# One load cut in two, and the last stores dealt out to other DMA engines, in a float32 matmul with bias and residual

## The chip, the cores and the metric

The kernel runs on 1 core of one Trainium2 chip. The metric is device time in microseconds (us), median of several runs. A ratio is the mean time of one kernel's runs over the mean of the other's runs of the same rounds, so it is not quite the ratio of the medians that are quoted beside it; it comes with a 95% interval.

A word on names. PE is the matmul engine, PEld its weight loads, DVE, ACT and POOL the vector, scalar and GpSimd engines, SP the queue that issues every transfer here. The *16 DMA engines* are the machines that move the bytes. A *landing* is the moment at which one of them adds its one to a transfer's semaphore: an evenly spread transfer has 16 of them, and the trace keeps their times, though not the engine's number.

## The reference

```python
x: (16, 512, 1024)  weight: (1024, 768)  bias: (768,)  residual: (16, 512, 768)   # float32
return np.matmul(x, weight) + bias + residual                                     # float32
```

The core must read 61.9 MB and write 25.2 MB; the profile's own account says so.

## The kernel before

The 8192 rows are 64 tiles of 128 rows, eight tiles to a *super tile* (S = 0 to 7). A row is on partition p and slot j, so a whole super tile of x (4 MB), residual or output (3 MB) moves in one transfer, with one long run of bytes per partition. A tile is cast to bf16 (ACT), transposed on PE, copied out of PSUM (DVE), multiplied, and added to residual and bias in place in the residual's buffer, from which it is stored. All transfers are issued by SP in the order of one list:

```python
# (kind, S, j0, j1[, cut]): x load, r residual load, s store, c store of one column chunk of one tile
ORDER = [('x', 0, 0, 2), ('w', 0, 0, 2), ...                                   # cut
 ('x', 1, 1, 4), ('r', 0, 4, 8), ('x', 1, 4, 8), ('r', 1, 2, 6), ('x', 2, 0, 8), ('r', 1, 6, 8),
 ...                                                                            # cut
 ('r', 6, 0, 8), ('s', 3, 0, 8), ('x', 7, 0, 8), ('r', 7, 0, 8), ('s', 4, 0, 8), ('s', 5, 0, 8), ('s', 6, 0, 8),
 ('s', 7, 3, 4, 108), ('s', 7, 0, 3), ('s', 7, 4, 6), ('s', 7, 6, 7), ('c', 7, 7, 0), ('c', 7, 7, 1)]
```

A store with a `cut` is issued as two transfers, the rows before and after it (here and in e12 below the wrapper `K_`, which keeps the order of the program, is left out):

```python
edges = [0, *cut, P]                       # P = 128
for p0, p1 in zip(edges, edges[1:]):
    nc.sync.dma_start(out=out_d[S, p0:p1, j0:j1, n0:n0 + nl],
                      in_=R[S % RO_SLOTS][p0:p1, j0:j1, n0:n0 + nl])
```

So before, tile 59 (S = 7, j = 3) is stored as 108 rows and 20 rows. The Trainium skill, "DMA: Bandwidth & Descriptors", section "Why a DMA increments its semaphore by 16 and not by 1", says that a transfer runs on k engines, k being the largest number up to 16 that divides its slowest dimension, and on the lowest-numbered k; an issuing sequencer writes the other 16 - k increments at once. The trace agrees on k: the 108-row store shows one early update and then 12 landings, the 20-row one 1 and 10. Thus 108 rows go as 9 rows to each of engines 0 to 11, 20 rows as 2 to each of 0 to 9, and engines 12 to 15 get no row of that tile. I call that *relief*: an even store gives every engine 8 rows. The numbers 0 to 15 here are labels by this rule; no trace prints them.

Of the kernel before, what the change touches and what calls it, by code (L numbers as in the profile page):

```python
# [28 lines left out]
 ('fin', 0), ('mm', 1, 3), ('mm', 2, 3)]  # L29
ORDER = [('x', 0, 0, 2), ('w', 0, 0, 2), ('x', 0, 2, 4), ('w', 1, 0, 2), ('b', 0, 0, 0), ('w', 2, 0, 2),  # L30
 ('w', 3, 0, 2), ('x', 0, 4, 6), ('r', 1, 0, 2), ('x', 0, 6, 8), ('r', 0, 0, 4), ('x', 1, 0, 1),
 ('x', 1, 1, 4), ('r', 0, 4, 8), ('x', 1, 4, 8), ('r', 1, 2, 6), ('x', 2, 0, 8), ('r', 1, 6, 8),
 ('r', 2, 0, 8), ('x', 3, 0, 8), ('s', 0, 0, 8), ('r', 3, 0, 8), ('x', 4, 0, 8), ('r', 4, 0, 8),
 ('s', 1, 0, 8), ('x', 5, 0, 8), ('r', 5, 0, 8), ('s', 2, 0, 8), ('x', 6, 0, 8), ('r', 6, 0, 8),
 ('s', 3, 0, 8), ('x', 7, 0, 8), ('r', 7, 0, 8), ('s', 4, 0, 8), ('s', 5, 0, 8), ('s', 6, 0, 8),
 ('s', 7, 3, 4, 108), ('s', 7, 0, 3), ('s', 7, 4, 6), ('s', 7, 6, 7), ('c', 7, 7, 0),
 ('c', 7, 7, 1)]
LAST = [(0, 512), (512, 256)]

# [256 lines left out]
```

## Time and profile before

| | before |
|---|---|
| median (range, runs) | 210.86 us (210.71 to 211.16, 6 runs) |
| span in the profile | 208.9 us |
| PE busy | 96% |
| DMA queue q1, share of 16 engines | 98.1% |
| last vector add ends | 204.8 us |
| landings of the very last store | 206.49 to 207.81 us |

Lines of the page of the kernel before: the span, the engines' busy time, the DMA engines' busy tenths and GB/s in 40 slices, the queues (packets, MB, share), and the chain that ended last, by engine.

```profile
span 208.9 us, 3104 instructions
...
PE 201.1 (96%) x1273; PEld 130.1 (62%) x1298; DVE 104.9 (50%) x140; ACT 67.2 (32%) x69; POOL 116.0 (56%) x72
...
DMA  6999999999999999999999999999999999999995
GB/s 234 426 429 413 415 434 436 418 457 404 443 430 460 398 419 441 453 408 431 424 433 435 438 433 409 463 424 411 452 414 439 414 433 441 428 428 420 419 395 205
...
q1 hardware_dynamic: 5918, 87.05, 98.1%
q8 instruction: 10, 0.16, 0.3%
q14 instruction: 4, 0.03, 0.0%
...
PE 76%; DMA 18%; ACT 1%; DVE 1%; issue 1%; SPq 0%; ACTq 0%
...
```

Two things are full at once: PE, and the DMA engines, whose row of tenths is 9 everywhere but at the two ends. 417 GB/s (87.05 MB in 208.9 us) fits the Trainium skill, "Perfetto Trace Analysis", section "Roofline", which puts a core alone at about 435 GB/s by its 16 DMA engines. The queue q8 is ten packets of 16 KB that are instructions, 0.3% of the time. (Queue q14 has four more in the span, of 8 KB and 0.3 us each.)

The place that the first half of the change aims at, in the timeline of the kernel before (start, us, engine, what; in brackets the idle time before it and who ended it), and in the waits between 40 and 60 us (in total, times, longest):

```profile
...
54.62 2.94 ACT L148 CAST xb<-x_tile 128x1024 bf16<-128x1024 f32 x3 [9.51 <-DMA x_tile<-in_x_dram]
55.72 0.42 PEld L156 LDWEIGHTS pt<-ident,xb 128*128 128x128 f32 x4 [0.48 <-ACT xb L148]
55.72 0.66 PE L156 MATMUL pt<-ident,xb 128*128 128x128 f32 x4
...
```

```profile
...
ACT xb L148 <- DMA x_tile<-in_x_dram: 15.2, 2, 9.5
...
PEld pt L156 <- ACT xb L148: 0.5, 1, 0.5
```

The cast of tile 16 waits until 54.62 us for the whole 4 MB of x of super tile 2, so PE's transposes start at 55.72 us. PE's transposes had come every 3.04 us (49.39, 52.43), so they were due at 55.47: 0.25 us late (0.3 at the next ones). No later wait of PE is of this kind.

The place that the second half aims at, the tail in the table of stretches of the kernel before (stretch in us, its length, busy times, granted clock, then DMA share and GB/s), and its small stores (KB each, us from issue to landing):

```profile
...
core 0: us, PE busy (x) PEld busy (x) DVE busy (x) ACT busy (x) POOL busy (x), PEclk, DMA share, GB/s
...
205.00:206.00 1.00, 0.00 (x0) 0.00 (x0) 0.00 (x0) 0.00 (x0) 0.00 (x0) 1.00 0.92 357
206.00:207.00 1.00, 0.00 (x0) 0.00 (x0) 0.00 (x0) 0.00 (x0) 0.00 (x0) 1.00 0.56 205
207.00:208.00 1.00, 0.00 (x0) 0.00 (x0) 0.00 (x0) 0.00 (x0) 0.00 (x0) 0.98 0.07 25
208.00:209.00 1.00, 0.00 (x0) 0.00 (x0) 0.00 (x0) 0.00 (x0) 0.00 (x0) 0.50 0.00 0
...
```

```profile
...
out_dram<-ro SPq DMA_DIRECT2D x1, 1152.0 KB, 8.0
out_dram<-ro SPq DMA_DIRECT2D x1, 768.0 KB, 5.2
...
out_dram<-ro SPq DMA_DIRECT2D x1, 384.0 KB, 4.1
out_dram<-ro SPq DMA_DIRECT2D x1, 324.0 KB
out_dram<-ro SPq DMA_DIRECT2D x1, 256.0 KB, 3.2
out_dram<-ro SPq DMA_DIRECT2D x1, 128.0 KB, 3.0
out_dram<-ro SPq DMA_DIRECT2D x1, 60.0 KB
...
```

After 204.8 us there is nothing left but stores, and the DMA share falls off gently: 0.92, 0.56, 0.07. If all 16 engines ended together it would fall at once. They do not, and the landings of the last store say how far apart they are (read from the trace, in order of time):

```
last store, before: 206.49 206.50 206.51 206.52 206.55 206.57 206.65 206.75 206.77 207.05 207.28 207.29 207.38 207.71 207.73 207.81
```

The lag is older than the tail. Here are landings of four big transfers, each 16 equal parts, with the 16 KB fetches that came between (the store of S=4, which lies between the second and the third, is left out):

```
x of S=7:        168.78 to 168.91 (4), 169.29 to 169.83 (4), 170.15 to 170.37 (7), 170.65
      16 KB instruction fetch at 176.7
residual of S=7: 176.08 to 176.21 (4), 176.59 to 177.13 (4), 177.44 to 177.65 (7), 179.45
store of S=5:    190.62 to 190.71 (4), 191.14, 191.15, 191.95 to 192.32 (9), 194.04
      16 KB instruction fetch at 196.3
store of S=6:    197.88 to 197.95 (4), 198.38, 198.39, 199.20 to 199.85 (8), 200.88, 201.28
```

Over the run the landings show eight engines that get such a jump, of about 1.5 us, one after each of the first eight fetches, and stay behind; the fetches at 176.7 and 196.3 us fall on two of these, which end 3.0 and 3.4 us behind the first (200.88 and 201.28 against 197.88). They are the *twice-hit* engines of this text. By following packets (chaining each to the one whose end meets its start) I found that all 16 engines run without a gap from 2 us to about 197 us at the earliest, 203.5 us for most, so a lag is not made up before the tail.

### The profile page before, as it was taken

The page shows a single profiled execution, that of the slowest core. Times are in us where ns is not written, and L with a number is a line of the kernel's source. Part 1 is how long each engine was busy: PE and PEld are TensorE (multiplying, and loading weights), DVE is VectorE, ACT ScalarE, POOL GpSimd, SP SyncE. Part 2 cuts the span into 40 slices and gives each one's busy share as a digit, 9 for nine tenths or more (in the row PEclk, how much of TensorE's full clock was granted, in tenths as well). Part 3 has the DMA queues.
Part 4 walks back from the last instruction along what each step waited for, and adds up shares of the span by engine and source line. Part 5 has one row for each costly group of instructions (what it writes and reads, how often), then busy time and mean ns, then how long its engine had stood idle before and what let it go on. Part 6 is the DMA issues. An engine that isn't in the chain of part 4 may idle for free.

```text
span 208.9 us, 3104 instructions
## 1 busy us (share of the span) xinstructions
PE 201.1 (96%) x1273; PEld 130.1 (62%) x1298; DVE 104.9 (50%) x140; ACT 67.2 (32%) x69; POOL 116.0 (56%) x72
## 2 busy tenths in 40 slices
PE   7999999999999999999999999999999999999991
PEld 2455666666666666666666666666666666666660
DVE  0457555427454644464554455455445544544551
ACT  2444325160563062422443054230724234430000
POOL 2100069999257990199589802994059910699100
PEclk9999999999999999999999999999999999999999
DMA  6999999999999999999999999999999999999995
GB/s 234 426 429 413 415 434 436 418 457 404 443 430 460 398 419 441 453 408 431 424 433 435 438 433 409 463 424 411 452 414 439 414 433 441 428 428 420 419 395 205
DMA packets 5932, 87.24 MB, mean 418 GB/s; under 512 B 666, under 2 KB 794, under 8 KB 2206
## 3 DMA queue, kind: packets, MB, share of 16 engines
q1 hardware_dynamic: 5918, 87.05, 98.1%
q8 instruction: 10, 0.16, 0.3%
q14 instruction: 4, 0.03, 0.0%
HBM read 61.88 MB, written 25.17 MB: 417 GB/s over the span
## 4 chain that ended last, share of the span: by engine, by line
PE 76%; DMA 18%; ACT 1%; DVE 1%; issue 1%; SPq 0%; ACTq 0%
PE psum_o L163 64%; DMA x_tile<-in_x_dram 18%; PE pt L156 11%; PE psum_o L257 1%; ACT xb L148 1%; DVE xt L157 1%; ACT xb L145 0%; DVE ro L261 0%; SPq L118 0%; SPq L121 0%; ACTq L148 0%
## 5 line engine op out<-in xcount | busy, mean ns | idle before, releaser
L163 PE MATMUL psum_o<-w_sb,xt 128*128 128x256 bf16 (+1 forms) x983 | 172.7, 324 | 1.7 <-DVE xt L157 0.3
L163 PEld LDWEIGHTS <-xt 128*128 128x128 bf16 x1008 | 98.5, 98 | 59.1 <-DVE xt L157 0.7
L188 POOL TENSOR_TENSOR ro<-ro,bias_sb 128x768 f32<-128x768 f32 x56 | 99.7, 1818 | 52.3 <-DMA ro<-in_residual_dram 52.3
L148 ACT CAST xb<-x_tile 128x1024 bf16<-128x1024 f32 x60 | 60.8, 1044 | 113.0 <-DMA x_tile<-in_x_dram 62.7
L157 DVE COPY xt<-pt 128x1024 bf16<-128x1024 bf16 x64 | 44.0, 691 | 76.9 <-PE pt L156 76.8
L198 DVE TENSOR_TENSOR ro<-psum_o,ro 128x768 f32<-128x768 f32 x55 | 52.3, 950 | 12.3 <-POOL ro L188 11.0
L156 PE MATMUL pt<-ident,xb 128*128 128x128 f32 x256 | 38.4, 274 | 0.3 <-ACT xb L145 0.2
L156 PEld LDWEIGHTS pt<-ident,xb 128*128 128x128 f32 x256 | 29.7, 141 | 9.3 <-ACT xb L145 1.1
L184 POOL TENSOR_TENSOR ro<-ro 128x768 f32<-128x768 f32 x8 | 14.3, 1822 | 19.4 <-DMA ro<-in_residual_dram 19.4
L194 DVE TENSOR_TENSOR ro<-psum_o,bias_sb 128x768 f32<-128x768 f32 x8 | 7.5, 948 | 0.0
L207 PE MATMUL psum_o<-warm 128*128 128x512 bf16 x12 | 5.3, 629 | 1.2 <-DVE warm_a L203 1.2
L228 ACT CAST w_sb<-ro 128x768 bf16<-128x768 f32 x4 | 3.3, 832 | 3.7 <-DMA ro<-in_weight_dram 3.7
L207 PEld LDWEIGHTS <-warm 128*128 128x128 bf16 x12 | 1.6, 141 | 4.0 <-issue 2.8
L228 POOL CAST w_sb<-ro 128x768 bf16<-128x768 f32 x1 | 0.8, 822 | 5.5 <-DMA ro<-in_weight_dram 5.5
L148 DVE CAST xb<-x_tile 128x1024 bf16<-128x1024 f32 x1 | 0.7, 696 | 4.4 <-DMA x_tile<-in_x_dram 4.4
L145 ACT CAST xb<-x_tile 128x512 bf16<-128x512 f32 x3 | 1.8, 616 | 3.4 <-PE psum_o L163 1.7
L257 PE MATMUL psum_o<-w_sb,xt 128*128 128x512 bf16 (+1 forms) x16 | 2.8, 326 | 0.0
L228 DVE CAST w_sb<-ro 128x768 bf16<-128x768 f32 x3 | 1.7, 558 | 2.0 <-DMA ro<-in_weight_dram 2.0
L146 DVE CAST xb<-x_tile 128x512 bf16<-128x512 f32 x3 | 1.2, 425 | 2.6 <-DMA x_tile<-in_x_dram 2.6
L257 PEld LDWEIGHTS <-xt 128*128 128x128 bf16 x16 | 1.6, 98 | 1.1
L222 PE MATMUL psum_o<-warm 128*128 128x512 bf16 x6 | 1.6, 379 | 0.0
L261 DVE TENSOR_TENSOR ro<-psum_o,ro 128x512 f32<-128x512 f32 (+1 forms) x2 | 1.1, 558 | 0.9 <-PE psum_o L257 0.8
(14 smaller groups left out, 5.1 us busy)
## 6 DMA issues: line engine op xcount, KB each, us to landing
x_tile<-in_x_dram SPq DMA_DIRECT2D x6, 4096.0 KB, 31.0
out_dram<-ro SPq DMA_DIRECT2D x7, 3072.0 KB, 24.7
ro<-in_residual_dram SPq DMA_DIRECT2D x6, 3072.0 KB, 21.4
ro<-in_residual_dram SPq DMA_DIRECT2D x3, 1536.0 KB, 22.2
x_tile<-in_x_dram SPq DMA_DIRECT2D x4, 1024.0 KB, 10.9
ro<-in_weight_dram SPq DMA_DIRECT2D x4, 768.0 KB, 9.7
x_tile<-in_x_dram SPq DMA_DIRECT2D x1, 2048.0 KB, 25.6
ro<-in_residual_dram SPq DMA_DIRECT2D x2, 768.0 KB, 21.5
```

What stands on the lines that cost most here:

```text
L145: K_(nc.scalar.copy(out=dst[:, 0:K // 2], in_=src[:, 0:K // 2]))
L148: K_((nc.scalar.copy if how == "s" else nc.vector.tensor_copy)(out=dst, in_=src))
L156: K_(nc.tensor.transpose(out=pt[:, q, :], in_=words[:, ts(q, P)], identity=ident))
L157: K_(nc.vector.tensor_copy(out=XT[t % XT_N].rearrange("p q m e -> p (q m e)"), in_=pt.rearrange("p q m -> p (q m)").bitcast(BF16),))
L163: K_(nc.tensor.matmul(PO[t % HEAD][:, n0:n0 + nl], lhsT=XT[t % XT_N][:, q, :, e], rhs=w_sb[:, q, e, n0:n0 + nl], start=(q == 0 and e == 0) ...
L184: K_(nc.gpsimd.tensor_add(out=r, in0=r, in1=tmp(t)))
L188: K_(nc.gpsimd.tensor_add(out=r, in0=r, in1=bias_sb))
L194: K_(nc.vector.tensor_add(out=tmp(t), in0=p, in1=bias_sb))
L198: K_(nc.vector.tensor_add(out=row(t), in0=p, in1=row(t)))
L207: K_(nc.tensor.matmul(PO[0][:, 0:512], lhsT=warm[:, 0:P], rhs=warm, start=True, stop=True))
L228: K_(copy(out=w_sb[:, q, e, :], in_=w_st[:, 2 * q + e, :]))
L257: K_(nc.tensor.matmul(p, lhsT=XT[t % XT_N][:, q, :, e], rhs=w_sb[:, q, e, n0:n0 + nl], start=(q == 0 and e == 0), stop=(q == n_q - 1 and e ...
```

## The change

Its intent: let PE begin super tile 2 when the first quarter of x is there; and spare two DMA engines more rows of the last stores. Tile 59 goes with tiles 56 to 60 in one even store, and tiles 61 and 62 are each stored as 126 rows and 2 rows. By the k rule 126 rows go as 9 to each of engines 0 to 13, and 2 rows as 1 to each of engines 0 and 1 (not to 14 and 15).

```diff
- ('x', 1, 1, 4), ('r', 0, 4, 8), ('x', 1, 4, 8), ('r', 1, 2, 6), ('x', 2, 0, 8), ('r', 1, 6, 8),
+ ('x', 1, 1, 4), ('r', 0, 4, 8), ('x', 1, 4, 8), ('r', 1, 2, 6), ('x', 2, 0, 2), ('x', 2, 2, 8),
+ ('r', 1, 6, 8),
  # cut: unchanged transfers, moved to other lines
- ('s', 7, 3, 4, 108), ('s', 7, 0, 3), ('s', 7, 4, 6), ('s', 7, 6, 7), ('c', 7, 7, 0),
+ ('s', 6, 0, 8), ('s', 7, 0, 5), ('s', 7, 5, 6, 126), ('s', 7, 6, 7, 126), ('c', 7, 7, 0),
  ('c', 7, 7, 1)]
```

No instruction of PE, DVE, ACT or POOL changes or moves; SP issues one transfer more.

## The prediction

> **What bounds the kernel now.** Two resources, both full. The page shows PE 96% busy and DMA queue q1 at 98.1% of the 16 engines' span, 417 GB/s. The chain of waits is almost all PE from 54.6 us on, but the end is a DMA: the last vector add ends at 204.8 us, the last store lands at 207.8, the span is 208.9.
>
> I followed packets in the trace, chaining each to the one whose end meets its start. Each of the 16 engines runs back to back from 2 us to about 203.5 us. They are not equally late: the store of super tile 6 ends between 197.4 and 200.9 us depending on the engine. The lag comes from ten 16 KB instruction fetches, each costing its engine about 1.35 us; two engines were hit twice. The last store lands on its engines between 206.5 and 207.8 us. The early ones wait for PE and the issue; the late ones were never idle.
>
> **x of super tile 2 in two transfers.** In the timeline the scalar cast at 54.62 us waits for the whole 4 MB of x (issued 24.5, landed 54.5), and the next transposes start about 0.3 us late against the 3.04 us tile pace; this is the only PE gap after the head. The first quarter lands some 7 us earlier, so the wait goes. PE, and both last stores' issue, move 0.3 us earlier. The late DMA engines do not care: their bytes are the same. One more issue (0.33 us on SP) and 8 more packets per engine cost almost nothing.
>
> **The tail stores.** The Trainium skill, "DMA: Bandwidth & Descriptors", section "Why a DMA increments its semaphore by 16 and not by 1", says a DMA uses the largest k up to 16 that divides its slowest dimension, on the lowest-numbered k engines. The trace agrees on k (the 108-row store lands in 12 steps, the 20-row one in 10); which engines, it does not show. So now, against an even 8 rows, engines 12-15 are spared 8 rows; after, 14-15 are spared 16, but 12-13 carry 18 rows instead of 16. One 3,072-byte row takes 118 ns. Against before: engines 2-9 lose a row (-0.1 us), 0-1 and 10-11 gain one, 14-15 lose 8 (-0.9), 12-13 gain 10 (+1.2 us).
>
> Which of 12-15 are late decides it. By row counts, among them are one engine never hit, one hit once, and the two hit twice, ending at 206.9 and 207.4 us. Fetches six and seven seem to fall on 10 and 11, eight to ten then on 12, 13, 14. If so the latest engine is 13: it ends 1.2 us later, and the kernel at 212.0. If the two are 14 and 15, the change saves 0.2 to 0.5 us. I hold the first likelier, 2 to 1.
>
> **Prediction.** 211.7 us, 8 in 10 between 210.2 and 212.3. Faster by over 2%: 0.01; within 2%: 0.97; slower by over 2%: 0.02.
>
> **What the profile should show.** No cast wait near 54.6 us, PE ending 0.3 us earlier; the 126-row stores landing in 14 steps, the 2-row ones in 2; the last store's 16 landings wider apart, the last near 209.0 against 207.8.
>
> **What would make it wrong.** The twice-hit engines being 14 and 15; fetches falling on other engines in the new program; the five-row store (issued at 197.7 us) leaving early engines dry; slow issue of small-k stores (the 20-row one took 0.89 us, the next 1.52) delaying the last two.

(The prediction's times of single engines are ends of packets. A landing comes a little later: the last packet of the kernel before ends at 207.40 us, its last landing is at 207.81.)

## The result, and the profile after

211.88 us (211.48 to 212.2, 6 runs) against 210.86; ratio 1.0046, interval [1.0031, 1.006]. The change makes the kernel slower by half a per cent, about 1 us, within the range forecast.

The page of the changed kernel, the same lines:

```profile
span 210.0 us, 3104 instructions
...
PE 200.2 (95%) x1273; PEld 130.0 (62%) x1298; DVE 104.8 (50%) x140; ACT 67.3 (32%) x69; POOL 116.0 (55%) x72
...
DMA  6999999999999999999999999999999999999994
GB/s 231 428 421 418 414 438 435 412 457 399 434 462 424 423 435 424 426 443 407 435 448 429 426 417 426 446 421 437 431 426 451 424 414 434 445 409 426 392 373 174
...
q1 hardware_dynamic: 5912, 87.05, 97.8%
q8 instruction: 10, 0.16, 0.3%
...
PE 88%; DMA 7%; SPq 2%; issue 1%; ACT 0%; DVE 0%; ACTq 0%
...
```

The totals hardly move; the DMA row's last digit is 4 instead of 5, the last slice 174 GB/s instead of 205. The first half of the change, in the timeline and the waits of the changed kernel between 40 and 60 us:

```profile
...
47.58 1.99 ACT L148 CAST xb<-x_tile 128x1024 bf16<-128x1024 f32 x2 [2.31 <-DMA x_tile<-in_x_dram]
...
54.89 2.94 ACT L148 CAST xb<-x_tile 128x1024 bf16<-128x1024 f32 x3 [5.32 <-DMA x_tile<-in_x_dram]
55.56 0.47 PEld L156 LDWEIGHTS pt<-ident,xb 128*128 128x128 f32 x4
55.67 0.60 PE L156 MATMUL pt<-ident,xb 128*128 128x128 f32 x4
...
```

```profile
...
ACT xb L148 <- DMA x_tile<-in_x_dram: 13.3, 3, 5.6
...
```

The first two tiles are cast at 47.58 us, long before they are needed; PE waits for no cast here (the line of PEld is gone from the waits) and the transposes come at 55.67, on the pace (49.60, 52.64). In this profile the head had been 0.2 us later, so the last PE work ends only 0.1 us earlier. The chain agrees: the DMA share of it fell from 18% to 7% and PE's rose from 76% to 88%, and yet the time grew. So the chain's shares do not say what the end waits for.

The tail, and the small stores:

```profile
...
core 0: us, PE busy (x) PEld busy (x) DVE busy (x) ACT busy (x) POOL busy (x), PEclk, DMA share, GB/s
...
205.00:206.00 1.00, 0.00 (x0) 0.00 (x0) 0.00 (x0) 0.00 (x0) 0.00 (x0) 1.00 0.88 309
206.00:207.00 1.00, 0.00 (x0) 0.00 (x0) 0.00 (x0) 0.00 (x0) 0.00 (x0) 0.62 0.87 330
207.00:208.00 1.00, 0.00 (x0) 0.00 (x0) 0.00 (x0) 0.00 (x0) 0.00 (x0) 0.50 0.44 161
208.00:209.00 1.00, 0.00 (x0) 0.00 (x0) 0.00 (x0) 0.00 (x0) 0.00 (x0) 0.50 0.07 24
...
```

```profile
...
out_dram<-ro SPq DMA_DIRECT2D x1, 1920.0 KB, 8.3
...
out_dram<-ro SPq DMA_DIRECT2D x2, 378.0 KB
...
out_dram<-ro SPq DMA_DIRECT2D x1, 256.0 KB, 4.4
out_dram<-ro SPq DMA_DIRECT2D x1, 128.0 KB, 4.1
out_dram<-ro SPq DMA_DIRECT2D x2, 6.0 KB
...
```

Between 206 and 208 us the DMA engines are now at 0.87 and 0.44 where they were at 0.56 and 0.07: the same bytes end later and further apart. The landings of the last store:

```
last store, after:  207.31 207.33 207.35 207.36 207.38 207.40 207.61 207.65 207.74 207.87 207.90 208.21 208.27 208.40 208.82 208.91
```

The last is 1.10 us later than before (208.91 against 207.81), which is the whole loss: the span grew by 1.1 us (208.9 to 210.0). The 126-row stores show 14 landings after one early update, the 2-row ones 2 after one. The 16 are a little wider apart, 1.60 us against 1.32, because the early landings are later too, by 0.8 us; whether that matters is asked below.

### The profile page after: what moved, and what is told of

It reads as the page before. It is cut to its first block, busy times and chain, and to the rows that moved or that the text cites. A ratio compares the mean times of both kernels' runs of the same rounds, so it can differ in the third digit from the quotient of the medians.

```text
span 210.0 us, 3104 instructions
## 1 busy us (share of the span) xinstructions
PE 200.2 (95%) x1273; PEld 130.0 (62%) x1298; DVE 104.8 (50%) x140; ACT 67.3 (32%) x69; POOL 116.0 (55%) x72
## 4 chain that ended last, share of the span: by engine, by line
PE 88%; DMA 7%; SPq 2%; issue 1%; ACT 0%; DVE 0%; ACTq 0%
PE psum_o L163 74%; PE pt L156 13%; DMA x_tile<-in_x_dram 7%; PE psum_o L257 1%; SPq L118 1%; SPq L121 0%; SPq L112 0%; ACT xb L145 0%; DVE ro L261 0%; ACTq L145 0%
## 5 line engine op out<-in xcount | busy, mean ns | idle before, releaser
L207 PE MATMUL psum_o<-warm 128*128 128x512 bf16 x12 | 4.6, 557 | 1.2 <-DVE warm_a L203 1.2
L222 PE MATMUL psum_o<-warm 128*128 128x512 bf16 x6 | 1.6, 379 | 0.0
```

What stands on the lines that cost most here:

```text
L207: K_(nc.tensor.matmul(PO[0][:, 0:512], lhsT=warm[:, 0:P], rhs=warm, start=True, stop=True))
```

## The experiments

Theory L (load): the end is the landing of the latest DMA engine; of the two twice-hit engines one is number 13, which the old cut spared 8 rows and the new one loads with 18 instead of 16. Its rivals: X, the cut load of x costs; I, the small stores on fewer than 16 engines are slow to issue, and this delays the end; H, the twice-hit engines are 14 and 15. All experiments change only the list of transfers, except the last.

| kernel | median us (runs) | ratio to before, interval | last landings in its profile |
|---|---|---|---|
| changed kernel | 211.88 (6) | 1.0046 [1.0031, 1.006] | 208.82, 208.91 |
| e1_x_only | 211.1 (5) | 1.0006 [0.9993, 1.0018] | 207.97, 208.04 |
| e2_tail_only | 212.17 (5) | 1.0051 [1.0036, 1.0065] | 208.22, 208.59 |
| e3_even | 211.74 (5) | 1.0033 [1.0021, 1.0046] | 208.50, 208.52 |
| e4_117 | 211.64 (5) | 1.0028 [1.0014, 1.0042] | 208.37, 208.50 |
| e6_before_even | 211.95 (6) | 1.0046 [1.0029, 1.0064] | 208.38, 208.58 |
| e7_112_16 | 211.63 (5) | 1.0037 [1.0024, 1.0051] | 208.22, 209.00 |
| e8_s6_126x2 | 211.65 (5) | 1.0043 [1.003, 1.0056] | 207.87, 208.82 |
| e9_s6_117 | 210.63 (5) | 0.9994 [0.9981, 1.0006] | 207.64, 207.75 |
| e10_s6_126 | 211.71 (5) | 1.0045 [1.0033, 1.0058] | 207.83, 209.02 |
| e11_s6_117x2 | 211.73 (6) | 1.001 [0.9986, 1.0035] | 207.88, 207.93 |
| e12_shift | 212.02 (4) | 1.0029 [1.0014, 1.0043] | 208.37, 208.51 |

The kernel before ran at 210.97 to 210.98 us beside e1 to e6, at 210.76 beside e7 to e10, and at 211.49 (210.69 to 211.76) beside e11 and e12, whose chip was slower and scattered more; compare by ratio. Each profile is one execution, often not the one with the median time. In these executions the device time is 2.7 to 3.2 us above the last landing, for both kernels and for all runs of the table: the time follows the last landing.

### e1_x_only and e2_tail_only: each half alone

```diff
 # e1, from before                      # e2, from before
-('x', 2, 0, 8)                         -('s', 7, 3, 4, 108), ('s', 7, 0, 3), ('s', 7, 4, 6), ('s', 7, 6, 7)
+('x', 2, 0, 2), ('x', 2, 2, 8)         +('s', 7, 0, 5), ('s', 7, 5, 6, 126), ('s', 7, 6, 7, 126)
```

> The kernel before with only x of super tile 2 split in two. Theory L (load: the span ends when the latest of the 16 DMA engines has moved its bytes, and the latest one, hit by two instruction fetches, is one of 12 and 13, which lost their relief): the split takes the 0.3 us PE wait near 54.6 us away but gives no time back, 210.6 to 210.9 us, ratio 0.998 to 1.000. Rival X (the split is what costs, by one more transfer and shifted semaphores): 211.5 to 212 us, ratio about 1.004.

> The kernel before with only the new tail stores. Theory L: 211.9 us, ratio 1.004 to 1.006, as the changed kernel. Rival X: 210.6 to 211.0. Rival I (the small-k stores issue slowly and delay the last two stores): also 211.9, so this run tells X from the other two only.

Measured: 1.0006 and 1.0051. The tail is the whole loss and rival X falls. In e1 the second-last store is issued at 203.99 us against 204.25 before: PE did gain its 0.26 us, and the kernel got nothing for it, because the last landing (208.04, against 207.81 in the profile of before) is that of an engine that had bytes to move anyway.

### e3_even: the changed kernel without any small store

```diff
-('s', 7, 5, 6, 126), ('s', 7, 6, 7, 126)
+('s', 7, 5, 6), ('s', 7, 6, 7)
```

> The changed kernel with tiles 61 and 62 stored evenly as 128 rows on 16 engines, no small-k store left. Theory L: engine 13 carries 16 rows instead of 18, 0.24 us less: 211.5 to 211.8 us, ratio about 1.0035. Rival I (issue of the small-k stores costs the microsecond): the loss is gone, 210.5 to 210.9 us. Rival H (the twice-hit engines are 14 and 15, which now lose a relief of 16 rows): 212.5 us or more unless those were not last.

Measured: 1.0033, as L said; rival I, for which the loss should be gone, falls as the explanation of most of it, and the 212.5 us or more of rival H did not come (211.74). The landings are the cleanest picture of the lags, because every engine carries the same:

```
last store, e3_even: 206.17 206.18 206.20 206.22 206.25 206.37 206.66 206.69 206.72 206.73 206.76 206.78 206.88 207.72 208.50 208.52
```

Thirteen engines end by 206.9, a *third latest* at 207.7, the two twice-hit ones at 208.5. Here is what the cuts are for.

### e6_before_even: the kernel before without its relief

```diff
-('s', 7, 3, 4, 108)
+('s', 7, 3, 4)
```

> The kernel before with tile 59 stored evenly as 128 rows on 16 engines, the relief taken away and nothing else. Theory L: engines 12 to 15 carry 8 rows more (0.93 us), the others up to 3 fewer: 211.5 to 211.8 us, ratio 1.003 to 1.0045. Rival I: small-k stores gone, issue faster (the 20-row one took 0.89 us, the next 1.52): 210.4 to 210.8 us.

Measured: 1.0046, just above the 1.003 to 1.0045 that L expected. The last two landings are 208.38 and 208.58, the third 207.61, the others at most 206.84. So the old cut was worth the microsecond: it takes the twice-hit two from 208.5 to 207.8, and pays with later ordinary engines. One transfer fewer and no small-k store did not help: rival I falls again.

### e4_117: the relief for three engines, in the tail

```diff
-('s', 7, 5, 6, 126), ('s', 7, 6, 7, 126)
+('s', 7, 5, 6, 117), ('s', 7, 6, 7, 117)
```

> The changed kernel with tiles 61 and 62 each stored as 117 rows on 13 engines and 11 rows on 11, which spares engines 13, 14 and 15 of 16 rows. Theory L with engine 13 the latest: engine 13 carries 18 rows less than in the changed kernel, and the latest is then one of the ordinary engines with one row more than in the kernel before: 210.6 to 211.1 us, ratio 0.999 to 1.001. Theory L with engine 12 the latest: no gain, 211.8 us. Rival I: four small-k stores remain, no gain, 211.8 to 212.2 us.

Measured: 1.0028: a miss. About four tenths of the loss seem recovered (1.0046 to 1.0028), but the two intervals overlap. The landings tell that the twice-hit engines were not last: their part of the five-row store landed at 205.89 and 205.99 us, 9 rows more take 1.06 us (9 x 118 ns), and no landing of the 117-row store is later than 206.06; so neither of the two was among its 13 engines. Other engines ended at 208.5. My sum had two holes: the third latest engine is not spared by this cut and carries 20 rows instead of 16 (4 x 118 ns = 0.47 us on its 207.7), and two pairs of small stores in the tail make everything later. (In this trace three packets of the five-row store, started after 202 us, took 1.10 to 1.40 us; the usual time is 0.57.) e11 below has the same rows without such pairs.

### e9_s6_117 and e10_s6_126: relief given earlier, to engines 13 to 15 or to 14 and 15

Both store super tile 7 evenly and cut one tile of super tile 6 instead, in a store that is issued at 182.2 us and lands near 200 us.

```diff
 # from e3
-('s', 6, 0, 8)
+('s', 6, 0, 7), ('s', 6, 7, 8, 117)        # e9;  e10 has 126
```

> Super tile 6 stored as seven tiles evenly and one tile as 117+11 rows, super tile 7 evenly; engines 13 to 15 are spared 8 rows, early enough that no small-k store is in the tail. Theory L with engine 13: the twice-hit two go from 208.5 to 207.6 us, and the third latest engine (207.7 with even stores) gets 2 rows and ends near 207.95: 210.9 to 211.1 us, ratio 0.999 to 1.001. With engine 12 twice hit instead: no gain, 211.7 to 212.0 us.

> As e9 but the one tile as 126+2 rows, which spares 14 and 15 alone. Theory L with engine 13: it keeps all its rows and gets one more, last landing about 208.6 us, 211.7 to 211.9 us, ratio 1.0035 to 1.0045. Rival H (14 and 15 twice hit): as e9, 210.8 to 211.1 us.

Measured: 0.9994 and 1.0045. This is the decisive pair: two kernels with the same number of transfers, the same shape of tail and nearly the same rows; the one difference that counts is whether engine 13 is spared. Rival H, that 14 and 15 are the twice-hit ones, falls. The tail of e9, then of e10, in the table of stretches:

```profile
...
core 0: us, PE busy (x) PEld busy (x) DVE busy (x) ACT busy (x) POOL busy (x), PEclk, DMA share, GB/s
...
205.00:206.00 1.00, 0.00 (x0) 0.00 (x0) 0.00 (x0) 0.00 (x0) 0.00 (x0) 1.00 0.99 383
206.00:207.00 1.00, 0.00 (x0) 0.00 (x0) 0.00 (x0) 0.00 (x0) 0.00 (x0) 1.00 0.46 168
207.00:208.00 1.00, 0.00 (x0) 0.00 (x0) 0.00 (x0) 0.00 (x0) 0.00 (x0) 1.00 0.04 14
208.00:209.00 1.00, 0.00 (x0) 0.00 (x0) 0.00 (x0) 0.00 (x0) 0.00 (x0) 0.56 0.00 0
...
```

```profile
...
core 0: us, PE busy (x) PEld busy (x) DVE busy (x) ACT busy (x) POOL busy (x), PEclk, DMA share, GB/s
...
205.00:206.00 1.00, 0.00 (x0) 0.00 (x0) 0.00 (x0) 0.00 (x0) 0.00 (x0) 1.00 0.97 377
206.00:207.00 1.00, 0.00 (x0) 0.00 (x0) 0.00 (x0) 0.00 (x0) 0.00 (x0) 0.67 0.62 233
207.00:208.00 1.00, 0.00 (x0) 0.00 (x0) 0.00 (x0) 0.00 (x0) 0.00 (x0) 0.50 0.11 39
208.00:209.00 1.00, 0.00 (x0) 0.00 (x0) 0.00 (x0) 0.00 (x0) 0.00 (x0) 0.50 0.05 16
...
```

In e10 the DMA engines are still at 0.05 in the last microsecond, about one engine of 16, and the landings show that it is one alone:

```
last store, e9_s6_117:   206.22 206.25 206.26 206.27 206.29 206.37 206.79 206.83 206.84 206.87 207.10 207.12 207.18 207.43 207.64 207.75
last store, e10_s6_126:  206.29 206.31 206.32 206.34 206.55 206.63 206.71 206.92 207.28 207.37 207.38 207.40 207.47 207.58 207.83 209.02
```

The cut stores say the same directly: the 14 landings of e10's 126-row store end with 199.97, 200.22 and then 201.63; the 13 of e9's 117-row store end with 199.71 and 200.04. One twice-hit engine is among the 14 and none among the 13.

### e8_s6_126x2: the loads of the changed kernel, earlier

```diff
 # from e3
-('s', 6, 0, 8)
+('s', 6, 0, 6), ('s', 6, 6, 7, 126), ('s', 6, 7, 8, 126)
```

> The rows of the changed kernel moved earlier: two tiles of super tile 6 are stored as 126+2 rows, super tile 7 evenly, so each engine carries what it carries in the changed kernel, but no small-k store is in the tail. Theory L (engine 13 twice hit and carrying 18 rows): last landing about 208.7 us, alone, the other twice-hit engine in time; 211.8 to 212.0 us, ratio 1.004 to 1.005. Rival I (small-k stores in the tail are the loss): 210.7 to 211.2 us, ratio at most 1.001. Rival H (14 and 15 twice hit): 210.7 to 211.0 us.

Measured: 1.0043, beside 1.0046 for the changed kernel. One landing at 208.82, alone, the next at 207.87. The same rows on the same engines cost the same when no cut store is in the tail.

### e7_112_16: as many small stores, all on 16 engines

```diff
 # from the changed kernel
-('s', 7, 5, 6, 126), ('s', 7, 6, 7, 126)
+('s', 7, 5, 6, 112), ('s', 7, 6, 7, 112)
```

> The changed kernel with tiles 61 and 62 each stored as 112 rows and 16 rows: as many stores as in the changed kernel, but every one on 16 engines and 8 rows an engine in all. If the number of small stores is what made the early engines late (their last landing 207.2 to 207.9 us against 206.2 to 206.9 with even stores), they are late here too, and the time is 211.8 to 212.1 us. If stores on fewer than 16 engines are the cause, the landings are as with even stores (the early ones 206.2 to 206.9 us, the twice-hit two at 208.5) and the time is 211.6 to 211.8 us, ratio 1.003 to 1.0035.

Measured: 1.0037, and the early landings are late, 207.16 to 207.42 us for the first ten, against 206.17 to 206.73 with even stores. So what makes the early engines late is that small stores follow each other, and not k: two of the four, the second of the first pair and the first of the second, took 1.24 and 1.23 us to issue (in e3 every store of the tail takes 0.33), and the last store's issue began at 205.40 us instead of 204.51. Packets stretch, too: in the profiles with such pairs in the tail (the changed kernel, e2, e4, e5, e7) the longest packet that starts after 202 us took 0.95 to 2.21 us, in all others at most 0.63. Why is not known. The time, though, is that of e3 within the intervals, since the twice-hit engine ends later still. Half of each of my two expectations came true: late early engines from the first, a time nearer the second.

### e11_s6_117x2: twice the relief of e9

```diff
 # from e9
-('s', 6, 0, 7), ('s', 6, 7, 8, 117)
+('s', 6, 0, 6), ('s', 6, 6, 7, 117), ('s', 6, 7, 8, 117)
```

> As e9 but two tiles of super tile 6 as 117+11 rows. Theory L: the twice-hit two, last in e9 at 207.64 and 207.75 us, lose 0.94 us more and end near 206.8; engines 0 to 10 get 2 rows more, so the third latest (207.43 in e9) ends near 207.67 and is the last: no real gain over e9, 210.4 to 210.7 us, ratio 0.998 to 1.000.

Measured: 1.001 with a wide interval, on the scattering chip. No gain over e9 is to be seen. In the profiled run, a quick one (210.66 us), the last landing is 207.93 us. Its engines carry the same rows as in e4, where the last was 208.50; the difference would be the pairs of small stores in the tail, but the intervals of the two ratios overlap, so this is only likely.

### e12_shift: moving the instruction fetches

From e9; the first 24 PE instructions (12 warm-up matmuls and their weight loads) become 224 tiny ones (here too the wrapper `K_` is left out).

```diff
-WARM = 12
+TINY = 112
-    for _ in range(WARM):
-        nc.tensor.matmul(PO[0][:, 0:512], lhsT=warm[:, 0:P], rhs=warm, start=True, stop=True)
+    for _ in range(TINY):
+        nc.tensor.matmul(PO[0][0:1, 0:1], lhsT=warm[:, 0:1], rhs=warm[:, 0:1], start=True, stop=True)
```

> e9 with the 12 warm-up matmuls replaced by 112 of one column, 200 more PE instructions at the head and no other work. If the 16 KB fetches are PE's instructions and make the lag of single engines, each comes some 15 us earlier (200 of 256 instructions a chunk, a chunk lasting 19.6 us), so the jumps seen between the landings around 179 and 200 us move to about 161 and 181 us, and an eleventh fetch falls near 201 us and makes one more engine late by 1.35 us, one without relief (it was hit near 60 us before): its last landing about 208.3 us, 211.1 to 211.5 us, ratio 1.001 to 1.004. If the lag has another cause, the jumps stay where they are, and the time is that of e9, 210.5 to 210.7 us, as long as PE itself is not later by over 1 us.

Measured: 1.0029. The 16 KB fetches moved with the PE instructions, and the jumps with them (times in us, from the trace):

```
                            e9_s6_117                        e12_shift
16 KB fetches (last four)   137.9, 157.7, 176.5, 195.8       142.9, 162.3, 182.5, 199.4  (11 in all, 10 in e9)
x of S=7, last two          170.44, 170.51                   170.50, 172.61
residual of S=7, last two   177.75, 179.36                   177.80, 179.89
last store, last four       207.18 207.43 207.64 207.75      208.12 208.16 208.37 208.51
```

That a fetch holds 256 PE instructions, as the expectation says, fits the trace: a tile has 40 of them and takes 3.04 us, which makes 258 in the 19.6 us between two fetches. In e12 one engine is 2.1 us behind the rest when x of S=7 lands, a transfer in which e9 has its last two 0.07 us apart: the jump came with the ninth fetch as in e9, but that fetch is now at 162.3 us instead of 176.5. (In e12 that engine had been 0.56 us behind one transfer earlier, 161.40 against 160.84, so the fetch at 162.3 us added about 1.55 us.) The eleventh fetch comes at 199.4 us, and the gain of e9 is gone. That it made an engine late that the cut does not spare is likely: the 11-row store, which goes only to engines that the cut loads, has its last landing at 201.09 us, against 200.24 in e9. One thing was not as wanted: PE ran some 1.4 us later in this kernel (the second-last store issued at 205.38 us instead of 203.96), so the early landings are 207.6 to 207.8 us. The two latest, at 208.4 and 208.5, are later than that, but a part of the loss may be PE's.

### e5_ident: a run that told nothing

The store of super tile 4 in five pieces, four of them cut, so that an engine's number could be read from its packets.

```diff
 # from the changed kernel
-('s', 4, 0, 8)
+('s', 4, 0, 4), ('s', 4, 4, 5, 120), ('s', 4, 5, 6, 126), ('s', 4, 6, 7, 117), ('s', 4, 7, 8, 108)
```

> The changed kernel with the store of super tile 4 cut into a half and four single tiles of 120+8, 126+2, 117+11 and 108+20 rows, so that the number of rows an engine moves there names it: engines 12, 13, 14 and 15 have 26, 17, 8 and 0 rows. Theory L: the packet chain with the instruction fetch near 176 us and an earlier one is engine 13 (17 rows), the one with the fetch near 196 us engine 14, and 15 has none. Rival H: they are 14 and 15. The time is not compared (some rows fewer on some engines), expected 211 to 213 us.

Measured: 214.53 us (one run, state unknown). The reading failed: the packets of small stores overlapped in ways my chaining could not follow. The time is a lesson of its own. The transfers take turns on eight semaphores, so each waits for the eighth before it to have landed; nine stores in the place of one moved the issue of the next big store from 161.9 to 185.2 us, and 15 of its 16 landings came within 0.75 us of each other (193.78 to 194.51): the engines had run dry (their busy share was 0.52 between 185 and 186 us) and started together. This is why e8 to e11 cut few stores.

## Why the prediction was right

- **Both PE and the DMA engines are full, and the end belongs to the latest DMA engine.** Right. e1 gave PE 0.26 us and the time did not move; e3, e6, e8, e9 and e10 moved only rows between DMA engines and the time followed the last landing: 207.8 to 208.0 us goes with medians of 210.6 to 211.1 us (the kernel before, e1, e9), 208.5 to 209.0 with 211.6 to 212.0 (the changed kernel, e3, e6, e8, e10).
- **The split of x removes a 0.3 us wait and is worth nothing.** Right (the cast wait is gone, ratio 1.0006). That PE ends 0.3 us earlier held in e1; in the changed kernel's own profile it was 0.1, the head of that run being 0.2 us later. There the issue of the last store did not move at all (204.79 us in both) and took longer, 1.30 us against 0.49.
- **k is 14 and 2.** Right, by 14 and 2 landings. That the 14 exclude one twice-hit engine and include the other is shown by e10; that the two rows do not go to engines 14 and 15 is fitting with it: in e10 they landed at 198.46 and 199.18 us, before either twice-hit engine had landed its share of the big store ahead of them (that store's last landings are 200.52 and 200.59), so neither of the two took one.
- **The twice-hit engine with the relief lost is 13.** Right, as far as labels by k go: it is spared by a cut of 117 and not by one of 126 (e9, e10). The argument by which I got there, fetches six and seven on engines 10 and 11 and so on in order, was not tested; it was a guess at two to one, with a saving of 0.2 to 0.5 us on the other side, so that the direction came out right is in part luck.
- **Its 10 rows more at 118 ns are 1.2 us.** Right: 1.10 us in the last landing, 1.0 us in the time.
- **The fetches make the lag.** e12 supports it: they are PE's instructions, since they moved with them, and the jumps moved too.
- **Not foreseen:** the early landings are 0.8 us later. I had named the slow issue of small stores only as a risk. It is real (e7). The rows alone are enough for the loss: e8, with the same rows and no cut store in the tail, is as slow. But in the changed kernel's own profile the small stores come close to being enough as well: a packet of the five-row store that starts at 203.14 us takes 2.21 us instead of 0.57. Its engine, not a late one until then, lands the five rows at 205.71 us, and by the time of its rows its last landing is the one at 208.82 us, only 0.09 us before the end. So relieving engine 13 alone in the tail would have saved that execution some 0.1 us; e4 (1.0028) fits.
- **The five-row store** did leave early engines dry, another risk named (DMA share 0.90 between 196 and 200 us, against 0.97), but e3, e9 and e10 have that store too (0.93, 0.90, 0.93), and e9 is as fast as the kernel before.

What stays open: why an issue right behind another often takes about 1 us. It is not a matter of small stores alone: in e6 an even store of 1,152 KB right behind one of 384 KB took 0.97 us, in e12 one of 3,072 KB took 1.26. Open too are why packets stretch beside the small stores of the tail, and how much of e4's time these two make. No version beats both kernels: e9 (0.9994) equals the kernel before, and is 0.5% faster than the changed one (0.9994 over 1.0046).

## What to carry to other kernels

When the DMA engines are full from start to end, the kernel ends with the latest of the 16, so read the 16 landing times of the last store before you move work between them: a mean share or the chain of waits does not show them. Uneven stores are a good tool to even out such lags, but they can spare only the engines that their divisor leaves out; check that the late ones are among these. It is safer to put the cut where the queue is deep than in the last stores, where pairs of small stores came with slow issues and stretched packets; that this shortens the time is likely (e11 against e4) and not shown. A wait that is removed on a second full engine can be worth nothing while the first one sets the end (e1).

## What the Trainium skill lacked or had wrong

- "Runtime: NRT & Kernel Launch", section "Instruction fetch mechanics", has the 16 KB blocks of 256 instructions and calls the cost of crossing one mostly hidden. For PE that holds here (96% busy, no wait of it begins at a fetch). It lacks that each block is carried by one of the engines that move the data: here it put that engine about 1.5 us further behind (at the fetch of 176.7 us from 0.28, 170.65 against 170.37, to 1.80, 179.45 against 177.65), for good, since it was never idle. Two hits on one engine set the end of the kernel.
- No page says on which DMA engine a fetch falls. Here the ninth and tenth fell on engines hit before, while other engines were not hit at all.
- "DMA: Bandwidth & Descriptors", section "Latency and other measured facts", says engines 7 and 15 are usually slower, as a guess by descriptor rings of GpSimd's transfers. No run here speaks against that guess or for it: this kernel issues everything from SP, and its two latest engines are explained by the fetches: 16 equal parts landed within 0.43 us of each other before the first fetch (5.08 to 5.51 us, first load), and 3.4 us apart at the end.
- The same page's rule of k held in every store looked at (126, 117, 108, 20 and 2 rows: 14, 13, 12, 10 and 2 landings), and e9 and e10 fit its "lowest-numbered" engines, though no trace prints a number.
- No page gives the issue time of a transfer right behind another: the second store of a pair took 0.3 to 1.2 us here, and an even one of 1,152 KB behind another 0.97 us (e6), against 0.33 us for most stores that come alone.
- No page has the stretched packets: with pairs of small stores in the tail single packets took 0.95 to 2.21 us, otherwise at most 0.63.
